# P7's weight subtraction of a chunk placed behind the low part of the product two places ahead of it

## The chip, the cores and the metric

The kernel runs on one core of one Trainium2 chip. The core has TensorE for matrix products (PE in the profile, its weight loads PEld), VectorE (DVE) and ScalarE (ACT) for elementwise work, GpSimd (POOL), SyncE (SP), which issues most of the DMA transfers, and 16 DMA engines. Each engine takes its instructions in the order of its own queue; between engines they wait for each other through semaphores. The metric is the device time of one execution in microseconds, as the median of several runs.

## The reference

Two layers of a hybrid encoder over 512 tokens of width 2048, in float32. A layer is an RMS norm, one input projection whose columns feed a gated linear attention group, a chunked softmax attention group and their gates, then one output projection and a second norm:

```
h = rmsnorm(x, g_pre)
z = h @ w_in                      # 2048 -> 7184
gq, gk, gv, gg, ga, aq, ak, av, ag = split_columns(z)
...
y = jnp.concatenate([o_gla, o_att], axis=-1) @ w_out
return x + rmsnorm(y, g_post)
```

Most of the work is in the two products with `w_in` and `w_out`.

## The kernel before

**Blocks.** The columns of `w_in` are cut into fourteen blocks of 512, those of `w_out` into four. A block of weights comes from memory in eight chunks of 512 KB, each a tile of 128 x 1024 float32 (two slices of 128 rows of the weights beside each other).

**Two parts.** A float32 product is made from three products of a faster format (fp32r): a chunk of weights `src` is cast to `wh` on ScalarE (L195), and VectorE subtracts to get the low part `wl = src - wh` (L199). The activations are held as high and low part in the same way. Per slice and output tile the PE then runs three matmuls: high x `wh`, high x `wl`, low x `wh`.

**Seven products instead of eight.** Six pairs of input blocks and the last pair of output blocks are computed by a Strassen-like scheme (`fast_gemm`): seven products P1 to P7 of sums of the weights with sums of the activations, each in four chunks c = 0 to 3. A product chunk (below: a product) is twelve matmuls of 128 x 512, or 24 of 128 x 256 where the output is laid out feature-major (L389). A pair runs, in this order, P1 x4, P5 x4, a mixture of P6 and P3, P7 x4, P2 x4, P4 x4; the last pair of a layer, called W23, runs P1, P2, P5, P6/P3, P7, P4. The weights of P5 and P6 are sums (`H = H + r`, L190), those of P7 are the difference `r = H - r` (L192), both on VectorE ahead of the cast. Outside the last pair P2 adds its weights to `H` behind its low part (L204). The sums of activations were stored to memory earlier and come back as tiles `sa` (L180).

**Buffers.** The loaded weights `raw` (`r` above), `H`, `wh` and `sa` have rings of four tiles, `wl` one of three. A load into `raw` waits until the tile's last reader is done; for P7 these are the low parts of P3, which read the tiles that P6 loaded. So P7's chunk 0 is loaded once the low part of P3's chunk 0 is done, seven products ahead of it, and its chunks 2 and 3 once those of P3's chunks 2 and 3 are done, four ahead.

**Order.** The program calls `load`, `high` and `low` of the coming products (`ahead`, L237) up to five, four and three places ahead of the one that the PE is at. A scheduler then sets each engine's queue from dependencies and its own estimate of times; `tc.issue_after(x)` forbids it to place an instruction ahead of `x`. The attention, gating and norm work is handed out between products (`pump`) and lands in the same queues, so an edit at one place can reorder other places.

**Between the layers.** The last block of layer 0's output projection, the residual sum (`finish_token`, L1243), the transposes of the new activations on PE (L541), their scaling on ScalarE (L554), the split into high and low part (L108, L109) and the first gate block of layer 1 (`std_gemm`, L314) run interleaved.

Of the kernel before, what the change touches and what calls it, by code (L numbers as in the profile page):

```python
# [11 lines left out]
ALU = mybir.AluOpType  # L12
# [22 lines left out]
def hybrid_trunk(  # L35
# [13 lines left out]
    nc = tc.nc  # L49
# [23 lines left out]
    def rtile(tag, shape=(2, W), dtype=F32, bufs=4):  # L73
        return ring.tile([P] + list(shape), dtype, tag=tag, name=nm(tag), bufs=bufs)
# [61 lines left out]
    LEFT = {"P5": "S1", "P6": "S2", "P3": "S4", "P7": "S3", "P4": "A22"}  # L136
    last_cast, last_load, last_low = [None], [None], [None]
    made = set()
    rows = {}

    class Job:
# [40 lines left out]
        def high(self):  # L182
            k, c, p = self.kind, self.c, self.pair
            if k == "std":
                src = self.raw
            else:
                h, r = p["H", c], p.get(("r", c))
                src = h if k in ("P1", "P5", "P6", "P4") else r
                if k in ("P5", "P6") or k == "P4" and self.b0 == W23[0]:
                    nc.vector.tensor_tensor(out=h, in0=h, in1=r, op=ALU.add)  # L190
                elif k == "P7":
                    nc.vector.tensor_tensor(out=r, in0=h, in1=r, op=ALU.subtract)  # L192
            self.src = src
            self.wh = rtile("wh", dtype=F32R)
            last_cast[0] = nc.scalar.copy(self.wh, src).ins  # L195

        def low(self):
            self.wl = rtile("wl", dtype=F32R, bufs=3)
            last_low[0] = nc.vector.tensor_tensor(  # L199
                out=self.wl, in0=self.src, in1=self.wh.bitcast(F32), op=ALU.subtract  # L200
            ).ins
            if self.kind == "P2" and self.b0 != W23[0]:
                h = self.pair["H", self.c]
                nc.vector.tensor_tensor(out=h, in0=h, in1=self.src, op=ALU.add)  # L204
# [1153 lines left out]
```

## Time and profile before

| | |
|---|---|
| runs, median (lowest to highest) | 1667.8 us (1666.9 to 1672.28), 3 runs |
| the profiled execution's own time | 1665.86 us |
| its span, first to last instruction | 1664.1 us |
| DVE busy | 1226.4 us (74%) |
| ACT busy | 901.4 us (54%) |
| DMA | 470.64 MB, mean 283 GB/s |

A row of a group reads: line, engine, operation, output <- inputs, size, count, then busy time and mean ns of one, then the idle time of the engine ahead of these instructions and what ended it. A row of the timeline reads: start, duration, engine, line, operation, count, and in brackets the idle time ahead of it with what ended it. Matmuls are pipelined: one of 128 x 512 shows a duration of 0.39 us, but the next starts about 0.23 us after it, so a PE that is shown as busy may have lost a little time that only the starts show. Names are the program's tile names without their numbers.

### The profile page before, as it was taken

Reading aid. Unit: us, or ns where it says so; the run is one execution under the profiler, and the core shown is the slowest. Engines: PE = TensorE matmul, PEld = TensorE weight load, DVE = VectorE, ACT = ScalarE, POOL = GpSimd, SP = SyncE. Lnnn points to the kernel's source line nnn. Section 1 sums busy time; section 2 is a strip of 40 time slices with the busy share of each in tenths; the row PEclk is TensorE's granted clock in tenths of the full one; section 3 lists DMA queues with packets and bytes.
Section 4 is the critical chain, followed back from the end, with each engine's and each line's share of the span. In section 5 each row is a group of like instructions: output and inputs, shape, how many; then the busy total and the mean of one; then the engine's idle time right before and its main releaser. Section 6 shows DMA issues by size and latency. Waiting matters only on the chain.

```text
span 1664.1 us, 24933 instructions
## 1 busy us (share of the span) xinstructions
PE 1634.7 (98%) x9030; PEld 1396.2 (84%) x9030; DVE 1226.4 (74%) x1595; ACT 901.4 (54%) x1499; POOL 166.5 (10%) x260
## 2 busy tenths in 40 slices
PE   9999999999999999999999999999999999999997
PEld 7888889999988877687888878899999888777776
DVE  7566776877876876678886676768778778856787
ACT  7444544565766544454784445445567665445443
POOL 1210000000100101310122000000010011013101
PEclk9999999999999999999999999999999999999999
DMA  9979786868867788798889687868587677878986
GB/s 378 343 269 321 282 305 232 301 188 301 280 193 271 276 322 265 272 337 302 292 290 399 221 331 258 312 224 297 193 312 249 223 275 287 298 240 302 347 291 234
DMA packets 150779, 470.64 MB, mean 283 GB/s; under 512 B 16428, under 2 KB 35636, under 8 KB 150656
## 3 DMA queue, kind: packets, MB, share of 16 engines
q1 hardware_dynamic: 127632, 389.36, 67.7%
q0 software_dynamic: 22304, 78.41, 12.3%
q8 instruction: 71, 1.16, 0.3%
q10 hardware_dynamic: 720, 1.28, 0.2%
q14 instruction: 52, 0.43, 0.1%
HBM read 396.88 MB, written 72.11 MB: 282 GB/s over the span
## 4 chain that ended last, share of the span: by engine, by line
PE 89%; DMA 6%; DVE 3%; issue 1%; ACT 1%; POOL 0%; DVEq 0%; SPq 0%; ACTq 0%; POOLq 0%
PE mm L399 41%; PE mm L314 19%; PE mm L389 18%; DMA raw<-in_w_dram 3%; PE ax L875 2%; DVE wl L199 1%; DMA t<-fg 1%; PE ax L858 1%; PE ax L1037 1%; PE ax L706 1%; DMA sa<-S 1%; PE ax L1071 1%; PE ax L836 1%; PE ax L838 1%; PE ax L837 1%
## 5 line engine op out<-in xcount | busy, mean ns | idle before, releaser
L399 PE MATMUL mm<-wh,sa 128*128 128x512 f32 x1536 | 487.7, 392 | 5.6 <-ACT wh L195 3.5
L195 ACT CAST wh<-raw 128x1024 fp32r<-128x1024 f32 x256 | 269.4, 1055 | 253.4 <-PE mm L399 84.7
L199 DVE TENSOR_TENSOR wl<-raw,wh 128x1024 fp32r<-128x1024 f32 x256 | 311.3, 1218 | 91.7 <-PE mm L314 30.9
L195 ACT CAST wh<-H 128x1024 fp32r<-128x1024 f32 x224 | 234.8, 1051 | 217.9 <-PE mm L399 122.3
L399 PEld LDWEIGHTS mm<-wh,sa 128*128 128x128 f32 x1536 | 288.6, 188 | 68.5 <-ACT wh L195 6.4
L199 DVE TENSOR_TENSOR wl<-H,wh 128x1024 fp32r<-128x1024 f32 x224 | 272.7, 1221 | 79.8 <-PE mm L399 29.8
L399 PE MATMUL mm<-wl,sa 128*128 128x512 f32 x768 | 301.5, 393 | 4.7 <-DVE wl L199 4.7
L389 PE MATMUL mm<-sa,wh 128*128 128x256 f32 x1280 | 238.1, 285 | 0.0
L389 PEld LDWEIGHTS mm<-sa,wh 128*128 128x128 f32 x1280 | 200.3, 191 | 0.5
L399 PE MATMUL mm<-wh,a 128*128 128x512 f32 x576 | 184.6, 392 | 0.0
L389 PE MATMUL mm<-sa,wl 128*128 128x256 f32 x640 | 181.3, 283 | 0.2 <-DVE wl L199 0.2
L399 PEld LDWEIGHTS mm<-wl,sa 128*128 128x128 f32 x768 | 144.6, 188 | 37.2 <-DVE wl L199 7.6
L314 PE MATMUL mm<-wh,a 128*128 128x512 f32 x512 | 172.3, 402 | 2.6 <-DVE g L1217 0.9
L190 DVE TENSOR_TENSOR H<-H,raw 128x1024 f32<-128x1024 f32 x120 | 145.7, 1220 | 11.2 <-DMA raw<-in_w_dram 9.5
L192 DVE TENSOR_TENSOR raw<-H,raw 128x1024 f32<-128x1024 f32 x56 | 68.6, 1225 | 82.4 <-DMA raw<-in_w_dram 82.2
L399 PEld LDWEIGHTS mm<-wh,a 128*128 128x128 f32 x576 | 108.0, 188 | 22.3
L437 POOL TENSOR_TENSOR sm<-sm,mhalf 128x4 f32<-128x4 f32 (+2 forms) x40 | 54.3, 1357 | 694.0 <-DVE sm L885 450.6
L389 PEld LDWEIGHTS mm<-sa,wl 128*128 128x128 f32 x640 | 122.4, 191 | 0.5 <-DVE wl L199 0.4
L314 PEld LDWEIGHTS mm<-wh,a 128*128 128x128 f32 x512 | 98.1, 192 | 26.1 <-DVE g L1217 1.8
L399 PE MATMUL mm<-wl,a 128*128 128x512 f32 x288 | 113.5, 394 | 0.0
L314 PE MATMUL mm<-wl,a 128*128 128x512 f32 x256 | 102.2, 399 | 0.0
L389 PE MATMUL mm<-a,wh 128*128 128x256 f32 x512 | 94.7, 284 | 0.0
(205 smaller groups left out, 2345.0 us busy)
## 6 DMA issues: line engine op xcount, KB each, us to landing
raw<-in_w_dram SPq DMA_DIRECT2D x320, 512.0 KB, 5.2
sa<-S SPq DMA_DIRECT2D x192, 512.0 KB, 4.8
H<-in_w_dram SPq DMA_DIRECT2D x56, 512.0 KB, 4.8
sa<-A SPq DMA_DIRECT2D x48, 512.0 KB, 5.5
S<-g POOLq DMA_DIRECT2D x32, 512.0 KB, 7.7
oS<-g POOLq DMA_DIRECT2D x32, 512.0 KB, 6.4
sa<-oS SPq DMA_DIRECT2D x32, 512.0 KB, 5.1
sg<-t POOLq DMA_DIRECT2D x32, 256.0 KB, 5.8
```

What stands on the lines that cost most here:

```text
L190: nc.vector.tensor_tensor(out=h, in0=h, in1=r, op=ALU.add)
L192: nc.vector.tensor_tensor(out=r, in0=h, in1=r, op=ALU.subtract)
L195: last_cast[0] = nc.scalar.copy(self.wh, src).ins
L199: last_low[0] = nc.vector.tensor_tensor(out=self.wl, in0=self.src, in1=self.wh.bitcast(F32), op=ALU.subtract).ins
L314: mm = nc.tensor.matmul(pss[o], a[:, part, t], rhs[:, kk, :], start=(i == 0 and kk == 0 and m == 0), stop=(i == n - 1 and kk == 1 and m == 2),
L389: nc.tensor.matmul(dst, lhs[:, kk, f], a[:, part, tok], start=(fresh and kk == 0 and m == 0 and ft % 2 == 0), stop=(c == 3 and kk == 1 and ...
L399: nc.tensor.matmul(out_ps[t], a[:, part, tok], rhs[:, kk, :], start=(fresh and kk == 0 and m == 0), stop=(c == 3 and kk == 1 and m == 2), ...
L437: nc.gpsimd.tensor_tensor(out=out_r, in0=v, in1=mhalf[:, : v.shape[-1]], op=ALU.pow)
L706: nc.tensor.matmul(ps[0:96, half * 256 : (half + 1) * 256], wga[kt // 10][:, kt % 10, :], op[:, i, (kt % 2) * 256 : (kt % 2 + 1) * 256], s ...
L836: nc.tensor.matmul(ps[:, :n], self.qh[:, t], self.kh[:, :n], start=True, stop=False)
L837: nc.tensor.matmul(ps[:, :n], self.qh[:, t], self.kl[:, :n], start=False, stop=False)
L875: nc.tensor.matmul(o, self.pt[i][:, j * P : (j + 1) * P], av[hd // 4, j // 2][:, j % 2, (hd % 4) * P : (hd % 4 + 1) * P], start=(j == 0), ...
```

## The change

The low parts are now listed as they are issued, and P7's difference may not stand ahead of the second last one.

```diff
@@ -136,6 +136,7 @@
     made = set()
+    lows = []
     rows = {}
@@ -189,7 +190,8 @@
                 elif k == "P7":
-                    nc.vector.tensor_tensor(out=r, in0=h, in1=r, op=ALU.subtract)
+                    with tc.issue_after(lows[-2]):
+                        nc.vector.tensor_tensor(out=r, in0=h, in1=r, op=ALU.subtract)
@@ -199,6 +201,7 @@
             last_low[0] = nc.vector.tensor_tensor(
                 out=self.wl, in0=self.src, in1=self.wh.bitcast(F32), op=ALU.subtract
             ).ins
+            lows.append(last_low[0])
```

When `high` of a product runs, the low parts up to the product just ahead of it have been issued, so `lows[-2]` is the low part two products ahead. The engines run the same instructions; their queues change in order alone. In the changed kernel L190 is L191, L192 is L194, L199 is L201, and lines behind them stand three lower.

**First place, VectorE, the second pair of layer 0.** Before, from P6's chunk 1 to P7's chunk 1; the tiles `raw_1961`, `raw_1982`, `raw_2003`, `raw_2028` are P7's four chunks, `wl_1998` and `wl_2023` the low parts of the first two of them:

```order
L199 TENSOR_TENSOR wl_1875<-H_1648,wh_1859 128x1024
L192 TENSOR_TENSOR raw_1961<-H_1620,raw_1961 128x1024
L199 TENSOR_TENSOR wl_1899<-raw_1840,wh_1877 128x1024
L192 TENSOR_TENSOR raw_1982<-H_1648,raw_1982 128x1024
L199 TENSOR_TENSOR wl_1920<-H_1666,wh_1902 128x1024
L199 TENSOR_TENSOR wl_1939<-H_1684,wh_1923 128x1024
L199 TENSOR_TENSOR wl_1957<-raw_1879,wh_1941 128x1024
L199 TENSOR_TENSOR wl_1977<-raw_1904,wh_1959 128x1024
L192 TENSOR_TENSOR raw_2003<-H_1666,raw_2003 128x1024
L199 TENSOR_TENSOR wl_1998<-raw_1961,wh_1980 128x1024
L192 TENSOR_TENSOR raw_2028<-H_1684,raw_2028 128x1024
L199 TENSOR_TENSOR wl_2023<-raw_1982,wh_2001 128x1024
```

And in the changed kernel:

```order
L201 TENSOR_TENSOR wl_1875<-H_1648,wh_1859 128x1024
L201 TENSOR_TENSOR wl_1899<-raw_1840,wh_1877 128x1024
L201 TENSOR_TENSOR wl_1920<-H_1666,wh_1902 128x1024
L201 TENSOR_TENSOR wl_1939<-H_1684,wh_1923 128x1024
L201 TENSOR_TENSOR wl_1957<-raw_1879,wh_1941 128x1024
L194 TENSOR_TENSOR raw_1961<-H_1620,raw_1961 128x1024
L201 TENSOR_TENSOR wl_1977<-raw_1904,wh_1959 128x1024
L194 TENSOR_TENSOR raw_1982<-H_1648,raw_1982 128x1024
L201 TENSOR_TENSOR wl_1998<-raw_1961,wh_1980 128x1024
L194 TENSOR_TENSOR raw_2003<-H_1666,raw_2003 128x1024
L201 TENSOR_TENSOR wl_2023<-raw_1982,wh_2001 128x1024
L194 TENSOR_TENSOR raw_2028<-H_1684,raw_2028 128x1024
```

The first two differences moved behind three or four low parts, the last two behind one. The first three pairs of both layers and the W23 pairs read like this; in the attention pairs other work stands between.

**Second place, VectorE, the W23 pair of layer 1, from the third low part of P2 to the second of P5.** `raw_15363` is what P5's chunk 1 adds to `H`; `wl_15379` and `wl_15400` are the low parts of P5's chunks 0 and 1. Before:

```order
L199 TENSOR_TENSOR wl_15332<-raw_15300,wh_15316 128x1024
L190 TENSOR_TENSOR H_15145<-H_15145,raw_15336 128x1024
L199 TENSOR_TENSOR wl_15358<-raw_15318,wh_15334 128x1024
L199 TENSOR_TENSOR wl_15379<-H_15145,wh_15361 128x1024
L190 TENSOR_TENSOR H_15168<-H_15168,raw_15363 128x1024
L199 TENSOR_TENSOR wl_15400<-H_15168,wh_15382 128x1024
```

And in the changed kernel:

```order
L201 TENSOR_TENSOR wl_15332<-raw_15300,wh_15316 128x1024
L191 TENSOR_TENSOR H_15145<-H_15145,raw_15336 128x1024
L201 TENSOR_TENSOR wl_15358<-raw_15318,wh_15334 128x1024
L191 TENSOR_TENSOR H_15168<-H_15168,raw_15363 128x1024
L201 TENSOR_TENSOR wl_15379<-H_15145,wh_15361 128x1024
L201 TENSOR_TENSOR wl_15400<-H_15168,wh_15382 128x1024
```

The second sum of P5 moved ahead of the low part of P5's first chunk. On SyncE's queue the load of `raw_15363` moved ahead of the load of an activation sum (`sa_15386`) at the same place:

```order
L147 DMA raw_15336<-in_w_dram 128x1024
L180 DMA sa_15365<-oS_141 128x1024
L180 DMA sa_15386<-oS_142 128x1024
L147 DMA raw_15363<-in_w_dram 128x1024
L180 DMA sa_15407<-oS_143 128x1024
```

In the changed kernel the same five read:

```order
L148 DMA raw_15336<-in_w_dram 128x1024
L181 DMA sa_15365<-oS_141 128x1024
L148 DMA raw_15363<-in_w_dram 128x1024
L181 DMA sa_15386<-oS_142 128x1024
L181 DMA sa_15407<-oS_143 128x1024
```

So the third and the fourth changed places. VectorE's queue a little ahead of this place moved too: one subtraction of an activation sum (L603) that waits for a load stands behind a low part and a product with the gain instead of ahead of them.

**Third place, PE, between the layers.** `ax_8318` is the first tile of transposed activations of the second half of the tokens; `wh_8266` and `wh_8290` are the sixth and seventh product of the first gate block of layer 1 (two output tiles, twelve matmuls each). Before, the transposes that complete that tile stand behind two matmuls of the sixth (`wh_8244` is the fifth):

```order
L314 MATMUL mm_8225<-wh_8244,a_1574_8029 128x512
L314 MATMUL mm_8224<-wh_8266,a_1576_8039 128x512
L314 MATMUL mm_8225<-wh_8266,a_1576_8039 128x512
L541 MATMUL ax_8318<-cst,bias_7083 128x128
L541 MATMUL ax_8318<-cst,g_1362_7079 128x128
```

In the changed kernel they stand behind nine of the seventh, the last three of which are shown:

```order
L317 MATMUL mm_8224<-wh_8290,a_1579_8056 128x512
L317 MATMUL mm_8225<-wl_8312,a_1579_8056 128x512
L317 MATMUL mm_8225<-wh_8290,a_1579_8056 128x512
L544 MATMUL ax_8318<-cst,bias_7083 128x128
L544 MATMUL ax_8318<-cst,g_1362_7079 128x128
```

So they moved back by ten matmuls of the sixth product and nine of the seventh. The scaling and splitting of these tiles on ScalarE and VectorE, the residual sums of the last token tile, the stores of sums on GpSimd and the matmuls of the forget gate (L706) moved with them.

## The prediction

> **What bounds the kernel now.** I read the page's busy times and its chain first, then the waits of all engines, then the places where PE waits for a low part.
>
> ```profile
> span 1664.1 us, 24933 instructions
> PE 1634.7 (98%) x9030; PEld 1396.2 (84%) x9030; DVE 1226.4 (74%) x1595; ACT 901.4 (54%) x1499; POOL 166.5 (10%) x260
> PE 89%; DMA 6%; DVE 3%; issue 1%; ACT 1%; POOL 0%; DVEq 0%; SPq 0%; ACTq 0%; POOLq 0%
> 214.39 43.36 PE mm L399 x190
> 257.75 67.43 PE mm L389 x562
> ```
>
> PE bounds it. The last two rows are undisturbed stretches of the chain: a 128x512 matmul starts every 43.36/190 = 0.228 us, a 128x256 every 67.43/562 = 0.120 us, so a product of twelve takes 2.74 us. An edit of VectorE's order can only give back time in which PE stands still. These rows of the table of waits (total, times, longest) bound that; the last one is the group of the moved subtractions:
>
> ```profile
> DVE raw L192 <- DMA raw<-in_w_dram: 82.2, 50, 4.5
> PE mm L399 <- DVE wl L199: 4.7, 6, 1.0
> PE mm L399 <- ACT wh L195: 3.5, 3, 1.7
> PE mm L389 <- DVE wl L199: 0.2, 1, 0.2
> L192 DVE TENSOR_TENSOR raw<-H,raw 128x1024 f32<-128x1024 f32 x56 | 68.6, 1225 | 82.4 <-DMA raw<-in_w_dram 82.2
> ```
>
> VectorE stands 82.2 us at the head of its queue for P7's loads, 50 times of 56, with low parts behind it. Yet PE waits for low parts only seven times, 4.9 us in all. Of 82.2 us nearly everything is hidden by the low parts' lead on PE; those 4.9 us, with what restarts cost, are what can be won.
>
> **The change, part by part.**
>
> **1. P7's stalls.** The second pair of layer 0 on SyncE's, VectorE's and PE's timelines:
>
> ```profile
> 200.88 0.33 SPq L147 DMA_DIRECT2D raw<-in_w_dram  x1
> 206.04 1.22 DVE L192 TENSOR_TENSOR raw<-H,raw 128x1024 f32<-128x1024 f32 x1 [2.46 <-DMA raw<-in_w_dram]
> 207.18 1.22 DVE L199 TENSOR_TENSOR wl<-raw,wh 128x1024 fp32r<-128x1024 f32 x1
> 208.43 0.33 SPq L147 DMA_DIRECT2D raw<-in_w_dram  x1
> 211.97 1.23 DVE L192 TENSOR_TENSOR raw<-H,raw 128x1024 f32<-128x1024 f32 x1 [3.57 <-DMA raw<-in_w_dram]
> 213.12 2.35 DVE L199 TENSOR_TENSOR wl<-H,wh 128x1024 fp32r<-128x1024 f32 x2
> 212.96 0.84 PE L399 MATMUL mm<-wh,sa 128*128 128x512 f32 x3
> 214.39 0.50 PE L399 MATMUL mm<-wl,sa 128*128 128x512 f32 x1 [0.59 <-DVE wl L199]
> ```
>
> The load issued at 200.88 lands and the difference runs at 206.04. Behind it stands the low part at 207.18, the last reader of the tile that the next load fills: that load goes out at 208.43, as it ends. The second difference waits for it until 211.97, and the low part behind that one ends too late: PE's matmul should start at 212.96 + 3 x 0.228 = 213.64 and starts at 214.39, 0.75 us late. The change takes both differences out from ahead of these low parts. Three more places of this shape, each the two rows of PE around the wait:
>
> ```profile
> 961.59 0.84 PE L399 MATMUL mm<-wh,sa 128*128 128x512 f32 x3
> 963.48 0.50 PE L399 MATMUL mm<-wl,sa 128*128 128x512 f32 x1 [1.05 <-DVE wl L199]
> 1039.09 0.84 PE L399 MATMUL mm<-wh,sa 128*128 128x512 f32 x3
> 1040.46 0.50 PE L399 MATMUL mm<-wl,sa 128*128 128x512 f32 x1 [0.53 <-DVE wl L199]
> 1138.40 0.40 PE L389 MATMUL mm<-sa,wh 128*128 128x256 f32 x2
> 1139.02 0.39 PE L389 MATMUL mm<-sa,wl 128*128 128x256 f32 x1 [0.22 <-DVE wl L199]
> ```
>
> By starts: 963.48 - 962.27 = 1.21, 1040.46 - 1039.77 = 0.69, 1139.02 - 1138.64 = 0.38. With 0.75 that is 3.03 us. The first matmul behind each wait shows 0.50 or 0.39 us where its like take 0.39 or 0.28: 0.11 each, 0.44 in all. Together 3.5 us; the gaps alone (0.59, 1.05, 0.53, 0.22) give 2.4. I take 3.5, because PE's starts are what the next work follows.
>
> Does the new place cost anything? With four `wh` and three `wl` tiles, a low part can start when PE has finished the product three ahead of it, and a cast when PE has finished the one four ahead. So, unblocked, the low part ahead of the difference of product i (that of i-2) starts as PE starts i-4; the difference ends 1.23 + 1.23 = 2.5 us later, and its cast may not start before 2.74. The low part of i normally starts as PE starts i-2, and is wanted 2 x 2.74 + 0.23 us after that: its spare is 5.71 - 1.23 = 4.5 us. The first two loads have had four or five products to land. The last two are issued as a low part of P3 ends, 216.63 and 218.07 here, and their difference stands two products behind that, 5.5 us. A 512 KB load takes 5.2 us in the median and 10.9 in the longest of the rows below. So VectorE may still wait up to 5.4 us, 0.9 above the spare, in a place where nothing now suggests such a load. I take 0 and keep +1.
>
> **2. The last pair of layer 1.** PE's other long waits stand here, where the queues moved too:
>
> ```profile
> raw<-in_w_dram SPq DMA_DIRECT2D x320, 512.0 KB, 5.2
> 1553.60 0.69 DVE L603 TENSOR_TENSOR t<-t,t 128x512 f32<-128x512 f32 x1 [1.48 <-DMA t<-fg]
> 1562.18 0.87 SPq L180 DMA_DIRECT2D sa<-oS  x2
> 1563.19 10.86 DMA raw<-in_w_dram
> 1574.07 1.23 DVE L190 TENSOR_TENSOR H<-H,raw 128x1024 f32<-128x1024 f32 x1 [4.36 <-DMA raw<-in_w_dram]
> 1573.10 0.39 PE L399 MATMUL mm<-wl,sa 128*128 128x512 f32 x1
> 1576.50 0.73 PE L399 MATMUL mm<-wh,sa 128*128 128x512 f32 x2 [0.75 <-ACT wh L195]
> 1577.76 0.50 PE L399 MATMUL mm<-wl,sa 128*128 128x512 f32 x1 [0.53 <-DVE wl L199]
> 1581.97 0.73 PE L399 MATMUL mm<-wh,sa 128*128 128x512 f32 x2 [1.65 <-ACT wh L195]
> 1583.69 0.79 PE L399 MATMUL mm<-wl,sa 128*128 128x512 f32 x1 [0.99 <-DVE wl L199]
> 1570.00:1575.00 5.00, 5.00 (x24) 4.14 (x23) 0.93 (x1) 0.00 (x0) 0.00 (x0) 1.00 1.03 420
> 1583.00:1587.00 4.00, 3.31 (x8) 2.66 (x9) 4.00 (x5) 2.65 (x3) 0.00 (x0) 0.57 0.86 294
> ```
>
> The load of P5's second chunk takes 10.86 us behind two 512 KB loads of sums, with the DMA engines full (share 1.03 of the first window, 420 GB/s); all four waits follow from it. It now stands ahead of one of them. If the transfers are served in their order it gains 0.52 MB / 420 GB/s = 1.25 us; if they share, nothing. VectorE's order ahead also lets the low part that frees its tile end earlier, since the subtraction that waits 1.48 us for its load ahead of 1553.60 has gone behind another low part: 0 to 1.4 us. Together 0 to 2.7; I take 1.5, nearer to the first price. The low part of P5's first chunk now stands behind the sum that waits until 1574.07: PE will want it at 1573.10, as before, and get it at 1574.07 + 2 x 1.23 = 1576.5. Two products (5.5 us) after that PE is at 1582.0, still ahead of 1583.69, when the chain of sums lets it go on: nothing is added.
>
> The Trainium skill, DMA: Bandwidth & Descriptors, section on queues, rings and completion order, says that each DMA engine consumes the descriptors of SyncE's queue in ring order, though completions need not follow it. By it the swap is worth the 1.25 us; without it, the term is the second half alone.
>
> PE's granted clock is 0.57 in the window 1583 to 1587: it falls behind these waits, none longer than 1.65 us. If that goes, another 0.43 x 4 = 1.7 us is won. I count 0 and keep it for the lower end. The Trainium skill, TensorE: Matmul & The Clock Gate, on what happens at the gate, gives an idle window of about 3.4 us as the condition; the row shows the fall without one, so the trace speaks against it. By the page no clock would be won here, and the new wait of 3.4 us up to 1576.5 would be at its limit.
>
> **3. Between the layers.** Nineteen matmuls now stand ahead of the transposes that make the second half's operands:
>
> ```profile
> 845.17 0.27 PE L541 MATMUL ax<-cst,bias 128*128 128x128 f32 x1
> 846.49 1.56 ACT L554 ACTIVATE g<-ax,gcol 128x256 f32<-128x256 f32 x4
> 849.29 1.29 DVE L109 TENSOR_TENSOR g<-g,g 128x512 fp32r<-128x512 f32 x2
> 856.04 0.39 PE L314 MATMUL mm<-wh,g 128*128 128x512 f32 x1
> ```
>
> Transposes at 845.17 give an operand at 849.29 + 0.68 = 849.97 that PE uses at 856.04: 6.1 us to spare. They move by 19 x 0.228 = 4.3 us, and ScalarE scales two slices more ahead of its cast, 2 x 1.56/4 = 0.8. Spare left: 1.0 us, a little less as four transposes went behind that matmul. I take +0.5, bounds 0 and +3, as the following tiles hang on the same engines.
>
> **Sum.** -3.5 - 1.5 + 0.5 = -4.5 us. The profiled execution took 1665.86 us, 1.9 below the median; it becomes 1661.4, and the median of 1667.8 becomes 1663.3.
>
> **The rivals.**
>
> **All of the last pair's wait shrinks.** 2.7 instead of 1.5 and the half-speed stretch goes: 1.2 + 1.7 more, 1660.4; to 1659.9 if nothing is lost between the layers. For it: all four waits hang on one load. Against: that load may stay long with full DMA engines.
>
> **Only P7's stalls go.** The load at the end is served as late as before, or VectorE's second chain holds PE to 1583.69: 1667.8 - 3.5 + 0.5 = 1664.8, or 1665.9 if only the 2.4 us come back.
>
> **The change does nothing.** Something else releases PE at those four places: 1667.8. Against it: the profile names the low part each time, and VectorE's rows show it ending as PE starts.
>
> **Slower: the operands between the layers come late.** If transposes, scaling and splits slip by more than 6.1 us instead of 5, PE waits for the excess, and its clock can fall for another 1.7 us. Slip by 12 us, and 5.9 + 1.7 is lost while 5.0 is won: 1670.4. It takes over the gains from a slip of about 9.5 us on. For it: nearly the whole spare is used, and casts of later weights stand in the same ScalarE queue. Against: the order gives 5 us, not 12.
>
> **How the numbers follow.** About 0.3% (5.0 us) is what a measurement of this kernel can tell from no change. Forecast, 1661.5 to 1665: 0.50, of it 0.14 below 1662.8. All of the last pair: 0.20, faster. P7 alone: 0.18, same. Nothing: 0.05, same. Slower: 0.07, of it 0.05 past 1672.8. So faster 0.34, same 0.61, slower 0.05. The range leaves out about half of the first rival and the slower one: 1660 to 1668.
>
> **What would show it.** Right: VectorE's idle time ahead of the differences falls from 82.2 us to some 10 or 20; PE no longer waits at those four products; in the last pair the load lands in 9 to 10 us. Wrong: a new row of PE waiting for `wh` or an operand `g` between the layers; PE waits at P7's second or third chunk behind a difference; the load at the end still taking 10.9 us.

## The result and the profile after

The changed kernel takes 1659.72 us (median of 6 runs, 1656.25 to 1660.81), the kernel before 1670.16 us (6 runs, 1666.9 to 1672.28): a ratio of 0.9936, 95% interval 0.992 to 0.9951. It is 10.4 us faster; 4.5 us were forecast, and 1659.72 lies just below the range of 1660 to 1668. The profiled execution took 1656.25 us.

The page of the changed kernel: span, busy times, and shares of the chain that ended last:

```profile
span 1654.5 us, 24885 instructions
PE 1629.4 (98%) x9030; PEld 1394.9 (84%) x9030; DVE 1228.9 (74%) x1595; ACT 902.2 (55%) x1499; POOL 166.7 (10%) x260
PE 93%; DMA 3%; DVE 1%; issue 1%; ACT 1%; SPq 0%; DVEq 0%; POOL 0%; ACTq 0%; POOLq 0%
```

The work is the same, VectorE's even 2.5 us longer; the span is 9.6 us shorter and PE's share of the chain grew from 89% to 93%. PE's waits for low parts and casts in the products of `fast_gemm` in the changed kernel (total, times, longest), and its group of differences:

```profile
PE mm L402 <- DVE wl L201: 1.0, 1, 1.0
PE mm L402 <- ACT wh L197: 1.6, 1, 1.6
```
```profile
L194 DVE TENSOR_TENSOR raw<-H,raw 128x1024 f32<-128x1024 f32 x56 | 68.3, 1220 | 1.4 <-DMA raw<-in_w_dram 1.2
```

VectorE's idle time ahead of the differences fell from 82.2 us to 1.2, further than the 10 to 20 us expected. PE's waits for low parts fell from 4.7 us to 1.0, those for casts from 3.5 to 1.6, and the two that are left stand in the last pair of layer 0. At P7's four places there is none.

The last pair of layer 1 on SyncE's and VectorE's timelines of the changed kernel, and the chain that ended last in the same stretch:

```profile
1557.37 0.33 SPq L181 DMA_DIRECT2D sa<-oS  x1
1557.80 0.53 SPq L148 DMA_DIRECT2D raw<-in_w_dram  x1
1558.42 0.98 SPq L181 DMA_DIRECT2D sa<-oS  x2
1564.60 1.23 DVE L191 TENSOR_TENSOR H<-H,raw 128x1024 f32<-128x1024 f32 x1 [1.72 <-DMA raw<-in_w_dram]
1571.36 1.23 DVE L191 TENSOR_TENSOR H<-H,raw 128x1024 f32<-128x1024 f32 x1 [0.38 <-DMA raw<-in_w_dram]
```
```profile
1559.17 10.43 PE ax L402 x46
1569.60 5.89 PE mm L402 x26
1575.49 0.02 issue
1575.51 24.55 PE mm L402 x107
```

The load of P5's second chunk goes out behind one sum instead of two and its sum of weights starts 1564.60 - 1557.80 = 6.8 us later; before it was 10.9 us, and 9 to 10 us were named as the sign of a right forecast. The last row of VectorE is the sum of the third chunk. All four waits of PE are gone: the chain, which ran through that load and VectorE for 24 us before, stays on PE.

Where the time went is seen from PE's starts: for each matmul, how much later than usual for its form (0.227 us for 128x512) the next one starts, where that is over 0.06 us. Without these late starts both profiles leave 1603 us (1664.1 - 61.2, 1654.5 - 51.5). The sums by place, in us, with a second profile of each kernel, taken later:

| late starts of PE | before | before again | changed | changed again |
|---|---|---|---|---|
| P7's four places | 3.5 | 3.6 | 0 | 0 |
| last pair of layer 1, P5 | 6.4 | 6.2 | 0.3 | 0.1 |
| between the layers | 1.2 | 1.3 | 1.0 | 1.0 |
| last pair of layer 0, P5 | 2.8 | 5.6 | 4.9 | 3.5 |
| all other places | 47.3 | 48.1 | 45.3 | 49.3 |
| together | 61.2 | 64.8 | 51.5 | 53.9 |

The first row counts the four waits (3.0 and 3.2 us) with the 0.1 us by which the matmul behind each of them is late. The first two rows repeat and give 9.6 and 9.7 us. The last two places move by some us between two executions of one program, so the +2.1 and -2.0 us that they show between the first two profiles are not shown to be an effect of the change.

### The profile page after: what moved, and what is told of

Read it like the earlier page. It is cut to its first block, busy times and chain, and to the rows that moved or that the text cites. A ratio compares the mean times of both kernels' runs of the same rounds, so it can differ in the third digit from the quotient of the medians.

```text
span 1654.5 us, 24885 instructions
## 1 busy us (share of the span) xinstructions
PE 1629.4 (98%) x9030; PEld 1394.9 (84%) x9030; DVE 1228.9 (74%) x1595; ACT 902.2 (55%) x1499; POOL 166.7 (10%) x260
## 4 chain that ended last, share of the span: by engine, by line
PE 93%; DMA 3%; DVE 1%; issue 1%; ACT 1%; SPq 0%; DVEq 0%; POOL 0%; ACTq 0%; POOLq 0%
PE mm L402 44%; PE mm L317 20%; PE mm L392 19%; PE ax L878 2%; DMA t<-fg 1%; DMA raw<-in_w_dram 1%; PE ax L861 1%; PE ax L1040 1%; PE ax L1074 1%; PE ax L709 1%; DMA sa<-S 1%; PE ax L402 1%; PE ax L841 1%; PE ax L839 1%; PE ax L840 1%
## 5 line engine op out<-in xcount | busy, mean ns | idle before, releaser
L201 DVE TENSOR_TENSOR wl<-raw,wh 128x1024 fp32r<-128x1024 f32 x256 | 312.0, 1221 | 116.1 <-PE mm L402 37.4
L201 DVE TENSOR_TENSOR wl<-H,wh 128x1024 fp32r<-128x1024 f32 x224 | 273.0, 1221 | 112.7 <-PE mm L402 52.0
L191 DVE TENSOR_TENSOR H<-H,raw 128x1024 f32<-128x1024 f32 x120 | 145.9, 1220 | 9.4 <-DMA raw<-in_w_dram 7.8
L317 PE MATMUL mm<-wh,g 128*128 128x512 f32 x256 | 85.6, 395 | 1.7 <-ACT g L108 1.4
```

The lines of the kernel that those rows point to most:

```text
L201: last_low[0] = nc.vector.tensor_tensor(out=self.wl, in0=self.src, in1=self.wh.bitcast(F32), op=ALU.subtract).ins
L317: mm = nc.tensor.matmul(pss[o], a[:, part, t], rhs[:, kk, :], start=(i == 0 and kk == 0 and m == 0), stop=(i == n - 1 and kk == 1 and m == 2),
```

## The experiments

**Theory A**: two things were won, P7's stalls (some 3 us) and the whole wait of the last pair (6 us), the second because its load has one transfer fewer ahead of it on SyncE's queue. **Theory B**: that load was slow by chance. Within A: **A1**, the load's place on SyncE's queue counts; **A2**, VectorE's queue counts, which frees the load's tile earlier because the subtraction that waits 1.48 us for its own load (L603) went behind a low part.

**The kernel of before again** (no edit).

> The kernel of before once more, for a second profile. Theory A (the last pair's wait comes from the order of the queues): PE starts late again by 0.7, 1.2, 0.7 and 0.4 us at the four low parts behind P7's differences and by 6 to 6.5 us in the last pair of layer 1, where the load of P5's second chunk takes 10 to 11 us again; what differs elsewhere by over 1 us is the spread of a run. Theory B (that load was slow by chance of what the DMA engines were doing): the load and the wait in the last pair differ from the first profile by 2 us or more.

1667.16 us (8 runs; ratio to the 28 runs of before beside it 0.9984, 0.9968 to 1.0, for the same program). Its waits:

```profile
PE mm L399 <- DVE wl L199: 5.4, 8, 1.0
PE mm L399 <- ACT wh L195: 3.9, 4, 1.7
```

Late starts of 0.8, 1.1, 0.7 and 0.5 us at P7's places and of 6.2 us in the last pair; the load took 10.9 us again. B falls. The profile is 4.3 us longer than the first, 2.8 of it in the last pair of layer 0, where the change leaves the order of the loads as it was.

**The rule without, and with nothing but, the W23 pair of layer 0.** Of the fourteen groups of differences only that pair's four move the queues between the layers and those of the last pair of layer 1 ahead of its P7: without them these queues are those of before, and with them alone those of the changed kernel. So the change falls into two parts. The diffs of this section show the changed lines alone, and this one in a shorter form (the run lists the other thirteen groups by name).

```diff
-                    with tc.issue_after(lows[-2]):
+                    with tc.issue_after(lows[-2]) if (self.l, self.b0) != (0, W23[0]) else nullcontext():
```

> The rule for P7's difference in all groups but the W23 pair of layer 0; queues between the layers and in the last pair of layer 1 ahead of P7 stay as before. Theory A: only P7's four stalls go, 3.0 to 3.5 us, ratio 0.998; the last pair of layer 1 keeps its 6 us of late starts. Theory B: the last pair may lose its wait here too, ratio 0.994 to 0.995.

> The rule for the W23 pair of layer 0 alone: that moves the queues between the layers and those of the last pair of layer 1, and leaves P7's four stalls. Theory A: about 6 us faster, ratio 0.9955 to 0.997, all of it in the last pair of layer 1; the late starts at P7's four places stay, 3.0 us; nothing between the layers beyond 1 us. Theory B: no fixed gain in the last pair; ratio 0.999 to 1.001.

Without it: 1663.25 us, ratio 0.9964 (0.995 to 0.9977). With it alone (`==` for `!=`): 1663.03 us, 0.9954 (0.9936 to 0.9972). PE's waits without, and then alone:

```profile
PE mm L402 <- ACT wh L197: 3.3, 2, 1.7
...
PE mm L402 <- DVE wl L201: 2.7, 4, 1.0
```
```profile
PE mm L402 <- DVE wl L201: 4.5, 6, 1.0
```

Without that pair no late start is left at P7's places, and the last pair keeps 5.8 us. With it alone the last pair keeps 1.0 us, its load takes 6.2 us instead of the 9.7 of the run without, and stalls stay at two of P7's four places (2.3 us in starts of over 0.3 us late). As A has it; the first ratio is better than the expected 0.998, but its interval reaches to within 1 us of that. By the ratios the parts would be worth 6.0 and 7.7 us, more than the whole change; these figures are known to some 2 to 3 us each, so the split rests on PE's starts and not on them.

**The order of loads alone.** On the kernel of before the load of the sum for P5's third chunk is held behind that of P5's second weight chunk, in layer 1 (`p["second"]` is that load).

```diff
-                nc.sync.dma_start(flat(self.a), src)
+                with tc.issue_after(p["second"]) if self.l == 1 and end and (k, c) == ("P5", 2) else nullcontext():
+                    nc.sync.dma_start(flat(self.a), src)
```

> The kernel of before with one rule alone: in the last pair of layer 1 the load of the sum for P5's third chunk stands behind the load of P5's second weight chunk on SyncE (with it the second sum of P5 stands ahead of the first low part of P5 on VectorE, as in the changed kernel). VectorE's subtraction that waits 1.5 us for its own load ahead of it stays where it was. Theory A1 (the load's place on SyncE makes the wait): the load lands in 6.5 to 9.5 us instead of 10.9, PE's late starts in the last pair fall from 6.4 us to below 2, ratio 0.996 to 0.9975. Theory A2 (VectorE's earlier release of the tile makes it): the load goes out as late as before, late starts stay at 4 to 6.4 us, ratio 0.999 to 1.000.

1666.02 us, ratio 0.9975 (0.9963 to 0.9987). The load took 7.0 us, late starts in the last pair fell to 1.6 us. In this kernel VectorE's second sum of P5 also moved ahead of P5's first low part, as in the changed one. So a second version holds that sum where it was (`issue_after(lows[-1])` around it), and nothing but two entries of SyncE's queue differ from before:

> The kernel of before with those two entries of SyncE's queue exchanged and every other queue as it was: the load of the sum for P5's third chunk behind the load of P5's second weight chunk in the last pair of layer 1; VectorE's second sum of P5 stays behind the first low part of P5. Theory A (the place of the load on SyncE's queue is what counts): the load takes 6 to 7.5 us instead of 10.9, late starts of PE in the last pair 1 to 2.5 us instead of 6.2 to 6.4; ratio 0.996 to 0.9985. Rival (VectorE's exchange of the sum and the low part was needed as well): late starts of 4 us or more though the load is short.

1665.07 us, ratio 0.9968 (0.9952 to 0.9984). SyncE's, VectorE's and PE's timelines of this version (PE's row is its only wait in the stretch):

```profile
1564.35 0.33 SPq L184 DMA_DIRECT2D sa<-oS  x1
1565.36 0.33 SPq L148 DMA_DIRECT2D raw<-in_w_dram  x1
1565.78 0.91 SPq L184 DMA_DIRECT2D sa<-oS  x2
1571.98 1.23 DVE L195 TENSOR_TENSOR H<-H,raw 128x1024 f32<-128x1024 f32 x1 [0.34 <-DMA raw<-in_w_dram]
1578.23 1.23 DVE L195 TENSOR_TENSOR H<-H,raw 128x1024 f32<-128x1024 f32 x1 [0.68 <-DMA raw<-in_w_dram]
1582.38 0.50 PE L406 MATMUL mm<-wl,sa 128*128 128x512 f32 x1 [0.98 <-DVE wl L205]
```

The load goes out 9.6 us ahead of P5's first matmul, as before (9.7), and its sum starts 6.6 us later, not 10.9. Late starts: 1.8 us instead of 6.2 to 6.4. A1 holds for about 4.5 us of the last pair's 6. The wait that is left is the third chunk's: its sum (1578.23) waits for a load of its own and starts 3.3 us behind P5's first matmul. In the changed kernel the loads go out earlier, that of the second chunk 11.6 us ahead of P5's first matmul, and the third sum starts 1.9 us behind it. With the change for the W23 pair of layer 0 alone the second load goes out as early (11.6 us), but the third sum starts 2.7 us behind, and 0.9 us of that wait stays. So A2's part, put down to the earlier release, is 0.8 to 1.7 us, depending on the third load; it was not tried alone.

**Both sums behind the load.** Also `("P5", 1)`: the load has no sum ahead of it.

> The kernel of before with both sums behind the weight load in the last pair of layer 1 and nothing else. Theory A (the price is per 512 KB transfer ahead of the load on SyncE's queue, about 2.2 us each at that queue's own 243 GB/s): the load takes 4.5 to 5.5 us, against 7.0 with one transfer moved and 10.9 with none; late starts in the last pair fall below 1 us from 6.3 and 1.6; ratio 0.996 to 0.998. Rival (the straggling part of one transfer makes the wait, not the number of transfers): the load stays at 6.5 us or more.

1667.4 us, ratio 0.9982 (0.9968 to 0.9996), where 0.996 to 0.998 was expected. The load took 5.0 us, as expected, yet late starts were 2.7 us and not below 1, more than with one sum moved. VectorE's and PE's timelines:

```profile
1575.47 1.22 DVE L194 TENSOR_TENSOR H<-H,raw 128x1024 f32<-128x1024 f32 x1
1583.48 1.23 DVE L194 TENSOR_TENSOR H<-H,raw 128x1024 f32<-128x1024 f32 x1 [2.44 <-DMA raw<-in_w_dram]
1585.91 0.73 PE L405 MATMUL mm<-wh,sa 128*128 128x512 f32 x2 [0.90 <-ACT wh L200]
1587.63 0.50 PE L405 MATMUL mm<-wl,sa 128*128 128x512 f32 x1 [0.99 <-DVE wl L204]
```

VectorE no longer waits for the second sum's load (the row of 1575.47 has no wait), but for the third's, which now lies behind both transfers that were moved. The expected gain turned into a wait one chunk later.

**The same order in layer 0.** In the changed kernel the last pair of layer 0 has the old order: its load takes 9.7 us, PE starts 4.9 us late.

```diff
-                nc.sync.dma_start(flat(self.a), src)
+                with tc.issue_after(p["second"]) if end and (k, c) == ("P5", 2) else nullcontext():
+                    nc.sync.dma_start(flat(self.a), src)
```

> The changed kernel once more. Theory A: no late start at P7's four places, below 1 us of them in the last pair of layer 1, whose second load takes 6 to 7.5 us; ratio 0.992 to 0.9955. If the 6 us of the last pair were a matter of one run, late starts of 3 us or more come back there.

> The changed kernel, with the order of loads that the change made in the last pair of layer 1 also put into the last pair of layer 0: the load of the sum for P5's third chunk behind that of P5's second weight chunk. There, in the changed kernel, the weight load takes 9.8 us and PE starts late by 4.8 us. Theory A (one 512 KB transfer fewer ahead of that load is worth some 3.9 us of it): the load lands in 6 to 7 us, late starts in the last pair of layer 0 fall to 0 to 2 us, the kernel is 3 to 4.5 us faster than the changed one, ratio to before 0.989 to 0.992. Rival (the swap is worth the 1.25 us of the forecast, and layer 1 was won by VectorE's earlier release): late starts fall to 3 to 4 us, about 1 us faster than the changed kernel.

> As the run before, and the load of the sum for P5's second chunk stands behind that weight load too, in both layers. Theory A: the load lands in 4 to 5.5 us, 2 us sooner than with one transfer moved, but little is left to win, since PE no longer waits for it: within 1 us of the run before (ratio 0.988 to 0.992). If the sum then comes late, a new wait of PE for the landing of a sum stands in the last pairs, up to 2 us each.

> The kernel with the order of loads in both layers once more, since its first ratio (0.9921) and that of the changed kernel (0.9936 and 0.9937) are closer than their intervals. If the gain of 1.5 us over the changed kernel is real: ratio 0.991 to 0.993, late starts in the last pair of layer 0 at 2 to 3.5 us again (3.5 to 4.9 in the changed kernel). If not: 0.993 to 0.995 and 3.5 us or more.

The changed kernel again: 1657.16 us, 0.9937 (0.9923 to 0.9951). One sum moved in both layers: 1655.62 us, 0.9921 (0.9908 to 0.9934), and again 1654.39 us, 0.9908 (0.9889 to 0.9927). Both moved: 1656.77 us, 0.9931 (0.9914 to 0.9949). PE's waits in the last pair of layer 0, first in the changed kernel, then in the second run with one sum moved:

```profile
754.02 0.73 PE L402 MATMUL mm<-wh,sa 128*128 128x512 f32 x2 [1.64 <-ACT wh L197]
755.74 0.50 PE L402 MATMUL mm<-wl,sa 128*128 128x512 f32 x1 [0.99 <-DVE wl L201]
```
```profile
753.72 0.50 PE L405 MATMUL mm<-wl,sa 128*128 128x512 f32 x1 [0.97 <-DVE wl L204]
```

The load took 7.3 us both times with one sum moved, late starts there were 2.9 and 1.7 us against 4.9 and 3.5. At this place the order helps by 2 us, not the 3 to 4.5 expected: VectorE still frees the tile late, and the load goes out 8.9 and 10.0 us ahead of P5's first matmul (10.3 and 10.6 there in the changed kernel, 11.6 in its layer 1). This version has the lowest median; its two ratios are 2.5 to 4.8 us better than the changed kernel's two, but the intervals overlap. With both sums moved the ratio missed the expected 0.988 to 0.992: the load took 5.0 us in layer 0 and 5.5 in layer 1, as expected, but late starts of 2.3 and 1.2 us stayed.

The length of that load in all fourteen profiles, both layers, by how many 512 KB sums were listed between it and the weight load ahead of it:

| sums ahead | loads | issue to landing, us (median) |
|---|---|---|
| two | 14 | 9.4 to 10.9 (9.8) |
| one | 11 | 5.9 to 9.2 (6.8) |
| none | 3 | 5.0 to 5.5 (5.0) |

**How far back the difference has to stand.** Outside the W23 pairs, `lows[-4]` (two places nearer to the head) and `lows[-1]` (one place later) in place of `lows[-2]`:

```diff
-                    with tc.issue_after(lows[-2]):
+                    with tc.issue_after(lows[-2 if self.b0 == W23[0] else -4]):
```

> The changed kernel, but outside the W23 pairs P7's difference is held only behind the low part four places ahead, so it may stand two low parts nearer to the head of VectorE's queue. Theory A (P7's stalls come from the place of the difference): VectorE's idle time ahead of the differences rises from 1.2 us to 15 to 60 us, and some late starts at P7's low parts come back, 0.5 to 3 us in all; ratio 0.993 to 0.997. Rival (any order that is forced takes the stalls away): idle time below 5 us, no late start there.

> The changed kernel, but outside the W23 pairs P7's difference is held behind the low part just ahead of it, one place later than in the change. By the forecast's spare of 4.5 us a place of 2.74 us costs nothing: no wait of PE for a cast or low part of P7, idle time ahead of the differences 0 to 2 us, and within 2 us of the changed kernel where other queues do not move for the worse (they move in many places here); ratio 0.992 to 0.996. Rival (the place of the change is already at the edge): PE waits for P7's cast at several of the 48 differences, 0.5 us or more each, and the kernel is over 5 us slower than the changed one.

Four back: 1660.51 us, 0.994 (0.9921 to 0.996). VectorE's idle time came back in part, but no late start of over 0.3 us at P7's low parts:

```profile
DVE raw L194 <- DMA raw<-in_w_dram: 27.4, 18, 4.9
```

So the expected stalls did not return: 27 us of waiting are still hidden by the low parts' lead, 82 were not quite. One back: 1671.57 us, 1.0008 (0.9992 to 1.0025), all of the gain lost. VectorE's and ScalarE's timelines at the third pair's P7, and PE's wait that follows:

```profile
299.11 1.23 DVE L201 TENSOR_TENSOR wl<-raw,wh 128x1024 fp32r<-128x1024 f32 x1 [1.65 <-PE mm L392]
300.26 1.22 DVE L194 TENSOR_TENSOR raw<-H,raw 128x1024 f32<-128x1024 f32 x1
301.70 1.05 ACT L197 CAST wh<-raw 128x1024 fp32r<-128x1024 f32 x1
302.78 1.23 DVE L201 TENSOR_TENSOR wl<-raw,wh 128x1024 fp32r<-128x1024 f32 x1 [1.31 <-ACT wh L197]
303.93 1.22 DVE L194 TENSOR_TENSOR raw<-H,raw 128x1024 f32<-128x1024 f32 x1
306.31 1.22 DVE L201 TENSOR_TENSOR wl<-raw,wh 128x1024 fp32r<-128x1024 f32 x1 [1.17 <-ACT wh L197]
318.45 0.39 PE L392 MATMUL mm<-sa,wl 128*128 128x256 f32 x1 [1.20 <-DVE wl L201]
```
```profile
ACT wh L197 <- DVE raw L194: 58.2, 28, 4.0
```

With the difference right behind the low part ahead of it a loop closes: low part, difference, cast, and the next low part, which needs that cast. One turn takes 3.5 to 3.7 us (302.78 - 299.11, 306.31 - 302.78), and PE needs a product every 2.74 to 2.88. Late starts around P7 outside the W23 pairs rose by 7 us. The other 12 of the 19.7 us of late starts above the changed kernel's first profile (this version's profiled execution, 1678.11 us, is the slowest of its ten) lie elsewhere, 7.3 of them in the last pair of layer 1, whose loads fell back into the old order; this kernel's queues differ in many places, so the ratio alone would prove little.

## Why the prediction was too small

**What bounds the kernel** was right: with PE's late starts taken off, the fourteen profiles (two of before, two of the changed kernel, ten of the other versions) leave 1602 to 1605 us.

**P7's stalls** were right, in place and in size: 3.5 us forecast, 3.5 and 3.6 in the two profiles of before, none in any kernel that has the rule or its four-back form. That the new place costs nothing held too. The reasoning behind its spare did not: by 4.5 us of spare, one place later (2.74 us) would have been free. The spare was worked out for one difference by itself; four in a row, each behind the low part just ahead of it, make the loop above. With two places between them two products pass in one turn.

**The last pair of layer 1** is the step that failed, by size: 1.5 us forecast, 2.7 at most, 6.1 measured. The mechanism was the right one. Three prices of that term were too low, that of the load above all.

- *One 512 KB transfer fewer ahead of the load* was priced at the rate of all queues together, 0.52 MB / 420 GB/s = 1.25 us. SyncE's queue does not get all of it. The DMA view of before, from the load's issue to its landing (1563 to 1574 us), with packets and MB of SyncE's queue (q1) and of GpSimd's stores (q0):

```profile
DMA packets 1080, 3.98 MB, mean 362 GB/s; under 512 B 112, under 2 KB 112, under 8 KB 1079
...
q1 hardware_dynamic: 729, 2.67, 70.2%
q0 software_dynamic: 350, 1.29, 28.9%
```

  2.67 MB in 11 us is 243 GB/s, so 2.2 us for one transfer. That is still only about half of the 4.1 us by which the load became shorter; the rest is the late last part of the load that the last section shows. The rows that the prediction quoted would have said as much: 10.86 us with two sums ahead and 5.2 for the median load make (10.86 - 5.2)/2 = 2.8 each. Measured: 10.9 us with two, 6.6 to 7.0 with one and 5.0 with none, on the kernel of before. The Trainium skill, DMA: Bandwidth & Descriptors, section on queues, rings and completion order, says besides the ring order that each DMA engine takes turns between the queues that have work; the trace shows the sharing, with 243 of 362 GB/s for SyncE's queue, but not the turns themselves; the forecast had not used that part.
- *The earlier release of the tile* was bounded at 1.4 us; the load went out 11.6 us ahead of P5's first matmul instead of 9.7, 1.9 us earlier.
- *The half-speed stretch* behind these waits was counted at 0 and went with them. Of the 6.4 us of late starts, 4.6 are the four waits themselves and 1.8 that stretch and small ones.

Together the sum of weights started 6.0 us earlier for PE (1.2 us after P5's first matmul before, 4.8 us ahead of it now), and PE's lateness fell by 6.1. That the two agree is chance: the waits were worth 4.6 of the 6.1, and the rest went with the clock. Nor do all four hang on that load alone: in every profile with one sum ahead of it in layer 1 the first two were gone and the third was 0.3 us at most, but the fourth went only where the third sum also started within 2 us of P5's first matmul. That the low part of P5's first chunk stands behind the waiting sum cost nothing, as forecast.

**Between the layers** 0.5 us was forecast, and nothing was lost. PE's transposes, VectorE's split and PE's first use of it there:

```profile
850.48 0.27 PE L544 MATMUL ax<-cst,bias 128*128 128x128 f32 x1
853.84 0.69 DVE L109 TENSOR_TENSOR g<-g,g 128x512 fp32r<-128x512 f32 x1
856.47 0.48 PE L317 MATMUL mm<-wh,g 128*128 128x512 f32 x1
```

The spare is 856.47 - 853.84 - 0.69 = 1.9 us, against 6.1 before and 1.0 forecast: nearly used up, but not past.

Of the rivals, the one in which all of the last pair's wait shrinks is what happened; its price, 2.7 us and 1.7 for the clock, carried the same error of the load. By terms, profile against profile: P7 -3.5 (forecast -3.5), last pair -6.1 (-1.5), between the layers -0.2 (+0.5); the other places together +0.1 us.

## What to carry to other kernels

Price a place in a DMA queue by what a load takes alone and behind others in the same profile, or at least by that queue's own rate at that moment, not by the rate of all queues together; and where several waits hang on one late transfer, count all of them, and the clock behind them, as what it can give back. An instruction that waits at the head of an in-order queue can stand behind work that is wanted sooner, but where it feeds a chain that comes back to that queue, leave as many places as the chain is long: two were free here, one cost some 7 us. An edit of an order at one place moved the queues at another, 800 us later, and two thirds of the gain came from there: look for every place that moved, and measure them apart.

## What the runs showed of the hardware

**PE's clock.** Windows of the changed kernel in the last pair of layer 0, PE's granted clock in the third column from the end:

```profile
752.00:756.00 4.00, 1.37 (x5) 0.56 (x4) 4.00 (x5) 2.52 (x4) 0.00 (x0) 1.00 0.83 285
756.00:760.00 4.00, 4.00 (x12) 3.07 (x12) 4.00 (x4) 2.30 (x3) 0.00 (x0) 0.59 0.71 254
```

The clock falls behind waits of 1.6 and 1.0 us. In the fourteen profiles every half-speed stretch between the kernel's start and its last 9 us is 3.413 us long (once two of them in a row), and within a profile all of them begin on one grid of 3.413 us. How long PE stood still (its late starts) in the grid's window just ahead decides; windows from 12 us on that were not at half speed themselves:

| PE standing still in a window of 3.413 us | windows | followed by half speed |
|---|---|---|
| 1.0 to 1.94 us | about 130 | 0 |
| 1.95 to 2.03 us | 6 | 3 |
| 2.04 us and more | 29 | 29 |

So in these windows it is the sum of the waits that counts, some 2 us of 3.4, and where the grid happens to lie: the same wait of 2.04 us (L1105, near 694 us) brought half speed in one run of the fastest version and none in the other. Each stretch costs 1.7 us; the two profiles of before have three and two of them, those of the changed kernel two and three (one of these at 7 us). This is one reason why executions of one program differ by several us. The Trainium skill, TensorE: Matmul & The Clock Gate, on what happens at the gate, has the window of about 3.4 us and that it runs freely, and both are seen here; that the clock falls after an idle window is not what these rows show, since a window that is 60% idle is enough.

**One late sixteenth.** The landing of a load is told by sixteen marks on its semaphore. For the load of the last pair, in us after its issue, the eighth, the fifteenth and the last of them:

| | 8th | 15th | 16th |
|---|---|---|---|
| before | 8.0 | 9.0 | 10.9 |
| before again | 8.2 | 8.9 | 10.9 |
| order of loads pinned | 5.8 | 6.2 | 6.6 |
| changed | 5.4 | 6.6 | 6.8 |

The middle moved by 2.2 to 2.8 us, about one transfer at the queue's own rate; the rest of the 4 us is one part in sixteen that came 1.8 to 2.0 us behind the others in the kernel of before. In all 28 loads of the table above the eighth mark came after 7.7 to 8.5 us with two sums ahead, 5.3 to 5.8 with one and 3.7 to 4.3 with none, while the last came 0.0 to 2.7 us behind the fifteenth. So, by the medians of the eighth mark, a place on the queue had a steady price of 1.8 to 2.6 us here, and the last part added a varying one. Why that part was late was not tried and stays open.
